# Dense products of a four-layer trunk in plain float32 instead of in three single-pass products

## The chip, the cores and the metric

The kernel runs on one core of a Trainium2 chip. The metric is the device time of one execution in microseconds (us); lower is better. Before the change it is 1484.35 us, the median of three runs (1482.13, 1484.35 and 1486.35).

A core has five engines with queues of their own: TensorE (PE) multiplies matrices into PSUM, VectorE (DVE) and ScalarE (ACT) work element by element, GpSimd (POOL) does a little of both, and SyncE (SP) issues transfers. The profile shows TensorE twice: PE is the multiplication, PEld the load of the stationary operand that goes ahead of it.

## The reference

512 tokens of width 1024 go through two layers, each a token mixer and a feed-forward block, with a residual addition after each of the four:

```
u = rms_norm(h, mixer_norm[0]);  h = h + swa_sink_attention(u)        # 16 heads of 64, window 128
u = rms_norm(h, ffn_norm[0]);    h = h + conv_glu_ffn(u)              # 1024 -> 2 x 3072 -> 1024
u = rms_norm(h, mixer_norm[1]);  h = h + gated_deltanet(u)            # 1024 -> 6176, 16 value heads, 2048 -> 1024
u = rms_norm(h, ffn_norm[1]);    h = h + conv_glu_ffn(u)
```

All inputs, weights and the output are float32. The dense products (attention in and out, the two feed-forward blocks, the DeltaNet's in and out projections) hold most of the arithmetic.

## The kernel before, in words

The residual `h` and every activation lie transposed: 128 features on the partitions, 512 tokens along the free axis, so a tensor of width 1024 is eight tiles of 128x512. A dense product takes one weight tile (128x1024, eight k tiles of 128x128) as stationary operand and the eight activation tiles as moving operand, and adds the eight k tiles up in one PSUM bank. Only the attention's input projection is turned round: there 128x128 pieces of the activation are stationary and 128x256 pieces of the weight move.

Both operands of a dense product are split in two float32r parts, float32r being a second format of four bytes: `hi` is the value rounded to it, `lo` what is left. `weight` (lines 128 to 139) loads a weight tile (`raw`), ScalarE makes `whi` (L137) and VectorE `wlo` (L138); the activations are split in `norm_split` (L192, L193), `normalise` (L223, L224) and `split` (L143, L144). `mm3` (L146 to L150) issues three products for each k tile, hi by hi, hi by lo and lo by hi. The weight pool has three slots for each of `raw`, `whi` and `wlo`.

The remaining products of the kernel have plain float32 operands before and after: attention scores (L515) and values (L546), and in the DeltaNet the per-head recurrence (L1013 to L1074). Transposes (L427, L537, L574) go through TensorE too.

The order of work is fixed when the program is built. The dense loops call `pump` once per one or two k tiles, and `pump` lets the waiting generators (attention lanes, the recurrence, the preparation of heads) emit their next piece, so small float32 products are strewn among dense ones. A scheduler then fixes each engine's order. All weights and most of the DeltaNet's reloads go through SP's queue in order. `live` counts the tiles taken from the pool of 36 activation tiles, and an epilogue (L1102) waits while there is no room.

Of the kernel before, what the change touches and what calls it, by code (L numbers as in the profile page):

```python
# [17 lines left out]
P = 128  # L18
T = 512
NB = 4  # L20
# [50 lines left out]
class Builder:  # L71
    def __init__(self, tc, ctx, ins, out):
# [3 lines left out]
        self.wp = pool("wp", 3)  # L76
# [44 lines left out]
    def a2(self, dt=F32R):  # L121
        return self.big.tile([P, T], dt, tag="a2", name="a2")
# [5 lines left out]
    def weight(self, src, cols=1024, parts=1):  # L128
        nc = self.nc
# [3 lines left out]
        w = cols // parts  # L133
        for i in range(parts):
            s = slice(i * w, (i + 1) * w)
# [3 lines left out]
        return hi, lo  # L139

    def split(self, src, hi, lo):
        nc = self.nc
        nc.scalar.copy(hi, src)  # L143
        nc.vector.tensor_tensor(lo, src, hi.bitcast(F32), op=ALU.subtract)  # L144

    def mm3(self, ps, w, x, first, last):  # L146
        mm = self.nc.tensor.matmul
# [4 lines left out]
    def dense(self, ps, hi, lo, x, n=KT, w=P, grain=2):  # L152
        for k in range(n):
            s = slice(k * w, (k + 1) * w)
# [31 lines left out]
    def norm_split(self, h, m, gain):  # L186
        nc = self.nc
        if m == 0:
            self.u = []
        hi, lo = self.a2(), self.a2()  # L190
        g = self.col(gain + m)
        nc.scalar.activation(hi, h, AF.Copy, scale=g)  # L192
        nc.vector.scalar_tensor_tensor(lo, h, g, hi.bitcast(F32), op0=ALU.mult, op1=ALU.subtract)  # L193
        self.u.append((hi, lo))
# [21 lines left out]
    def normalise(self, h, m, gain):  # L216

        nc = self.nc
        t = self.t2()
        nc.vector.tensor_tensor(t, h, self.bc, op=ALU.mult)  # L220
        hi, lo = self.a2(), self.a2()
        g = self.col(gain + m)
        nc.scalar.activation(hi, t, AF.Copy, scale=g)  # L223
        nc.vector.scalar_tensor_tensor(lo, t, g, hi.bitcast(F32), op0=ALU.mult, op1=ALU.subtract)  # L224
        self.u.append((hi, lo))


    def ffn(self, l, h, after):
        nc = self.nc
        u = self.u  # L230
        for third in range(3):
            act = []
            for j in range(third * 8, third * 8 + 8):
                gu = []
                for b in range(2):
                    hi, lo = self.weight(self.ins["up"][l, j, b])
                    ps = self.psum()
                    self.dense(ps, hi, lo, u)
                    gu.append(ps)
# [10 lines left out]
                nc.vector.tensor_tensor(t, t, y, op=ALU.mult)  # L250
                hi, lo = self.a2(), self.a2()
                self.split(t, hi, lo)
                act.append((hi, lo))
            for m in range(KT):
                hi, lo = self.weight(self.ins["down"][l, third, m])
                ps = self.psum()
                self.dense(ps, hi, lo, act)
# [138 lines left out]
    def attn(self, h, after):  # L396
# [38 lines left out]
        def lane(i):  # L435
# [3 lines left out]
            for x in range(NB + 2):  # L439
                if x >= 2:  # L440
# [3 lines left out]
                    if n == 0:  # L444
                        ao[i] = [(self.a2(), self.a2()) for _ in range(4)]
# [5 lines left out]
                    for g in range(4):  # L451
                        s = slice(n * P, (n + 1) * P)
                        hi, lo = ao[i][g]
                        self.split(po[:, g * P:(g + 1) * P], hi[:, s], lo[:, s])
# [19 lines left out]
        for c in range(6):  # L474
# [3 lines left out]
            for i, (t, k) in enumerate(order):  # L478
                ts = slice(t * P, (t + 1) * P)
                ps = pss[t // 2][:, (t % 2) * 256:(t % 2) * 256 + 256] if c else pss[t][:, :256]  # L480
                hi, lo = W[k // 4]
                s = slice(k % 4 * 256, k % 4 * 256 + 256)
                self.mm3(ps, (u[k][0][:, ts], u[k][1][:, ts]), (hi[:, s], lo[:, s]), k == 0, k == KT - 1)
# [7 lines left out]
        for i in range(2):  # L491
            self.until(lambda: ("o", i) in ready)
            for m in range(KT):
                hi, lo = self.weight(self.ins["wout"][i, m], 512)
                ps = self.psum()
                self.dense(ps, hi, lo, ao[i], 4, grain=1)
# [53 lines left out]
    def in_tile(self, j, u):  # L550
        hi, lo = self.weight(self.ins["gin"][j])
        ps = self.psum()
        self.dense(ps, hi, lo, u, grain=1)
# [26 lines left out]
    def gates(self, u, ready):  # L580
# [19 lines left out]
        hi, lo = self.weight(self.ins["gba"], 256)  # L600
        ps = self.psum()
        for k in range(KT):
            s = slice(k * 32, (k + 1) * 32)
            self.mm3(ps[:32], (hi[:, s], lo[:, s]), u[k], k == 0, k == KT - 1)
# [49 lines left out]
        self.rows2 = [self.a2().rearrange("p (n c) -> p n c", n=NB) for _ in range(2)]  # L654
# [16 lines left out]
    def gdn(self, h, hd, stack, after):  # L671
# [68 lines left out]
        self.live, self.started = 26, 0  # L740
# [23 lines left out]
        def part(ps, m, W, q, ks):  # L764
            hi, lo = W
            for k in ks:
                s = slice((m % 2 * 4 + k) * P, (m % 2 * 4 + k + 1) * P)
                self.mm3(ps, (hi[:, s], lo[:, s]), outs[4 * q + k], k == 0, k == 3)
# [8 lines left out]
        while r < len(rest) or g < 12:  # L777
            q = g // 4
            if r < len(rest) and (r < 3 * self.started or not have(4 * q + 4)):
                tile_in(rest[r])  # L780
                r += 1
                if r == len(rest):
                    self.live -= 16
            elif have(4 * q + 4):
# [11 lines left out]
                if g % 4 == 0:  # L796
                    self.live -= 8
# [281 lines left out]
    def epilogue(self, rx, hk, mo, o, ready, outs):  # L1079
# [22 lines left out]
        while self.live + 4 > 36:  # L1102
            yield 0.5
        self.live += 4
        for j in range(2):
            pt = self.turn(ob[j])
            V.scalar_tensor_tensor(z[:, j], pt, self.col(C_GN), z[:, j], op0=ALU.mult, op1=ALU.mult)
            hi, lo = self.a2(), self.a2()
            self.split(z[:, j], hi, lo)
            outs[2 * hk + j] = (hi, lo)  # L1110
# [68 lines left out]
```

## Time and profile before

| what | us |
|---|---|
| median of three runs | 1484.35 |
| profiled execution | 1481.57 |
| its span, first to last instruction | 1479.8 |
| PE busy | 1466.2 |
| PEld busy | 1216.8 |
| DVE busy | 913.7 |
| ACT busy | 636.3 |
| POOL busy | 104.7 |

Matmuls are pipelined: the next one starts while the last is still draining, so the duration of one in a row of the profile is longer than the time it takes from the engine. What a matmul takes is read from the distance between one start and the next.

### The profile page before, as it was taken

How to read it: one execution, taken by the hardware profiler on the slowest of the kernel's cores; microseconds unless marked ns; L12 is line 12 of the kernel's file. 1: busy time of each engine (PE TensorE's matmuls, PEld its weight loads, DVE VectorE, ACT ScalarE, POOL GpSimd, SP SyncE). 2: the span in 40 equal slices, each digit the busy share in tenths (PEclk: the TensorE clock that was granted, in tenths of full speed). 3: DMA queues.
4: the chain of work that ended last, by engine and by line, in shares of the span. 5: the costliest groups of instructions: out<-in, count | busy, mean ns of one | idle time of the engine just before them, and what ended most of it. 6: DMA issues, size and time to landing. Idle time of an engine off the chain costs nothing.

```text
span 1479.8 us, 20837 instructions
## 1 busy us (share of the span) xinstructions
PE 1466.2 (99%) x7972; PEld 1216.8 (82%) x7972; DVE 913.7 (62%) x1772; ACT 636.3 (43%) x1206; POOL 104.7 (7%) x141
## 2 busy tenths in 40 slices
PE   8999999999999999999999999999999999999998
PEld 8976688888888888878888888888888888888887
DVE  8778765446635556765685667767685535644552
ACT  6666643223313334667534454454453313322331
POOL 0122100000000000000112222230000000000000
PEclk9999999999999999999999999999999999999999
DMA  5201222222222233356866445453222222222231
GB/s 188 72 19 60 82 98 100 100 100 100 86 99 100 100 121 121 118 174 229 278 230 210 150 142 174 154 162 122 73 101 98 100 100 100 88 98 100 100 106 65
DMA packets 70940, 178.14 MB, mean 120 GB/s; under 512 B 17208, under 2 KB 23352, under 8 KB 70584
## 3 DMA queue, kind: packets, MB, share of 16 engines
q1 hardware_dynamic: 61128, 158.70, 32.1%
q10 hardware_dynamic: 7920, 16.27, 2.9%
q0 software_dynamic: 1792, 1.84, 0.7%
q8 instruction: 63, 1.03, 0.3%
q14 instruction: 37, 0.30, 0.1%
HBM read 150.46 MB, written 26.31 MB: 119 GB/s over the span
## 4 chain that ended last, share of the span: by engine, by line
PE 93%; DVE 3%; DMA 3%; ACT 1%; issue 1%; POOL 0%; SPq 0%; ACTq 0%; DVEq 0%; POOLq 0%
PE ps L148 27%; PE ps L149 27%; PE ps L150 27%; PE ps L574 1%; PE ps L1061 1%; PE ps L1074 1%; PE ps L515 1%; PE ps L546 1%; PE ps L1067 1%; PE ps L1056 1%; PE ps L1052 1%; DVE wlo L138 1%; ACT sc L524 1%; PE ps L537 1%; DMA vd<-t 1%; PE ps L1027 1%
## 5 line engine op out<-in xcount | busy, mean ns | idle before, releaser
L148 PE MATMUL ps<-a,whi 128*128 128x512 f32 x1736 | 688.9, 397 | 0.4 <-ACT a L143 0.4
L150 PE MATMUL ps<-a,wlo 128*128 128x512 f32 x1736 | 677.1, 390 | 0.0
L149 PE MATMUL ps<-a,whi 128*128 128x512 f32 x1736 | 676.9, 390 | 0.0
L137 ACT CAST whi<-raw 128x1024 fp32r<-128x1024 f32 (+1 forms) x239 | 242.4, 1015 | 434.1 <-PE ps L149 389.9
L148 PEld LDWEIGHTS ps<-a,whi 128*128 128x128 f32 x1736 | 325.4, 188 | 70.5 <-issue 2.5
L150 PEld LDWEIGHTS ps<-a,wlo 128*128 128x128 f32 x1736 | 325.2, 187 | 69.3
L149 PEld LDWEIGHTS ps<-a,whi 128*128 128x128 f32 x1736 | 325.8, 188 | 64.0 <-DVE a L144 0.2
L138 DVE TENSOR_TENSOR wlo<-raw,whi 128x1024 fp32r<-128x1024 f32 (+1 forms) x239 | 282.1, 1181 | 68.1 <-ACT whi L137 67.6
L258 DVE TENSOR_TENSOR h<-h,ps 128x512 f32<-128x512 f32 x48 | 33.0, 688 | 148.5 <-PE ps L150 148.5
L243 DVE TENSOR_TENSOR t<-ps,rbc 128x512 f32<-128x512 f32 x48 | 33.2, 691 | 109.3 <-PE ps L150 103.9
L249 DVE TENSOR_TENSOR t<-ps,rbc 128x512 f32<-128x512 f32 x48 | 33.2, 691 | 86.4 <-PE ps L150 86.3
L247 ACT ACTIVATE t<-t 128x512 f32<-128x512 f32 x48 | 30.4, 632 | 97.8 <-DVE t L246 97.8
L148 PE MATMUL ps<-whi,a 128*128 128x256 f32 x192 | 56.9, 298 | 1.2 <-ACT a L192 1.2
L149 PE MATMUL ps<-wlo,a 128*128 128x256 f32 x192 | 54.0, 283 | 1.2 <-DVE wlo L138 1.2
L150 PE MATMUL ps<-whi,a 128*128 128x256 f32 x192 | 53.1, 283 | 0.0
L954 POOL MEMSET TT<- 128x1024 f32 x8 | 7.7, 958 | 562.8 <-DMA Xd<-kd 554.9
L143 ACT CAST a<-t 128x512 fp32r<-128x512 f32 x48 | 29.9, 624 | 32.6 <-DVE t L250 32.6
L148 PEld LDWEIGHTS ps<-whi,a 128*128 128x128 f32 x192 | 36.6, 191 | 7.6 <-issue 4.9
L566 DVE SCALAR_TENSOR_TENSOR t<-ps,cols,t 128x511 f32<-128x511 f32 (+2 forms) x48 | 35.7, 744 | 7.1 <-ACT t L564 6.5
L244 ACT ACTIVATE t<-t,cols 128x512 f32<-128x512 f32 x48 | 38.9, 810 | 0.0
L528 POOL TENSOR_SCALAR sc<-sc,sm 128x256 f32<-128x256 f32 (+1 forms) x32 | 28.9, 913 | 128.2 <-DVE sm L526 65.1
L149 PEld LDWEIGHTS ps<-wlo,a 128*128 128x128 f32 x192 | 36.6, 191 | 1.4 <-DVE wlo L138 1.4
(252 smaller groups left out, 1472.5 us busy)
## 6 DMA issues: line engine op xcount, KB each, us to landing
raw<-in_up SPq DMA_DIRECT2D x96, 512.0 KB, 3.2
raw<-in_down SPq DMA_DIRECT2D x48, 512.0 KB, 3.2
raw<-in_gin SPq DMA_DIRECT2D x48, 512.0 KB, 3.6
raw<-in_gout SPq DMA_DIRECT2D x16, 512.0 KB, 3.5
raw<-in_win SPq DMA_DIRECT2D x10, 512.0 KB, 3.1
raw<-in_wout SPq DMA_DIRECT2D x16, 256.0 KB, 2.7
zd<-t ACTq DMA_DIRECT2D x16, 256.0 KB, 3.0
Dd<-D ACTq DMA_DIRECT2D x8, 512.0 KB, 2.7
```

The costliest lines, as they stand in the source:

```text
L137: nc.scalar.copy(hi[:, s], raw[:, s])
L138: nc.vector.tensor_tensor(lo[:, s], raw[:, s], hi[:, s].bitcast(F32), op=ALU.subtract)
L143: nc.scalar.copy(hi, src)
L148: mm(ps, w[0], x[0], start=first, stop=False)
L149: mm(ps, w[0], x[1], start=False, stop=False)
L150: mm(ps, w[1], x[0], start=False, stop=last)
L243: nc.vector.tensor_tensor(g, gu[0], self.bc, op=ALU.mult)
L244: nc.scalar.activation(y, g, AF.Identity, bias=self.col(C_FB + l * 24 + j), scale=self.col(cw + 2))
L247: nc.scalar.activation(y, y, AF.Silu)
L249: nc.vector.tensor_tensor(t, gu[1], self.bc, op=ALU.mult)
L258: nc.vector.tensor_tensor(h[m], h[m], ps, op=ALU.add)
L566: nc.vector.scalar_tensor_tensor(dst[:, i:], g[:, :T - i], self.col(cw + 3 - i), dst[:, i:], op0=ALU.mult, op1=ALU.add)
```

## The change

Weights and activations of dense products stay plain float32. `weight` only loads; there is no `split`, no `mm3`, and one product per k tile. The pool of weight tiles has six slots of one kind where it had three of each of three kinds. An activation takes one tile, not two, and the counts of `live` are halved. The core of the diff:

```diff
-        self.wp = pool("wp", 3)
+        self.wp = pool("wp", 6)
-    def a2(self, dt=F32R):
+    def a2(self, dt=F32):
     def weight(self, src, cols=1024, parts=1):
-        raw = self.wp.tile([P, 1024], F32, tag="raw", name="raw")
-        hi = self.wp.tile([P, 1024], F32R, tag="whi", name="whi")
-        lo = self.wp.tile([P, 1024], F32R, tag="wlo", name="wlo")
+        w = self.wp.tile([P, 1024], F32, tag="w", name="w")
...
-            nc.sync.dma_start(raw[:, s], src[:, s])
-            nc.scalar.copy(hi[:, s], raw[:, s])
-            nc.vector.tensor_tensor(lo[:, s], raw[:, s], hi[:, s].bitcast(F32), op=ALU.subtract)
+            self.nc.sync.dma_start(w[:, s], src[:, s])
...
-        mm(ps, w[0], x[0], start=first, stop=False)
-        mm(ps, w[0], x[1], start=False, stop=False)
-        mm(ps, w[1], x[0], start=False, stop=last)
...
-            self.mm3(ps, (hi[:, s], lo[:, s]), x[k], k == 0, k == n - 1)
+            self.nc.tensor.matmul(ps, w[:, k * P:(k + 1) * P], x[k], start=k == 0, stop=k == n - 1)
...
     def normalise(self, h, m, gain):
-        nc.vector.tensor_tensor(t, h, self.bc, op=ALU.mult)
...
-        nc.scalar.activation(hi, t, AF.Copy, scale=g)
-        nc.vector.scalar_tensor_tensor(lo, t, g, hi.bitcast(F32), op0=ALU.mult, op1=ALU.subtract)
+        self.nc.vector.scalar_tensor_tensor(x, h, self.col(gain + m), self.bc, op0=ALU.mult, op1=ALU.mult)
...
     def ffn(self, l, h, after):
-                nc.vector.tensor_tensor(t, t, y, op=ALU.mult)
-                hi, lo = self.a2(), self.a2()
-                self.split(t, hi, lo)
+                x = self.a2()
+                nc.vector.tensor_tensor(x, t, y, op=ALU.mult)
...
-        self.live, self.started = 26, 0
+        self.live, self.started = 18, 0
```

On TensorE, around the first step of the DeltaNet's chain (`S` is the state of a head, `qd` the decayed queries, `a2` the activation tiles, `whi`, `wlo` the parts of a weight), the kernel before has:

```order
L148 MATMUL ps_7241<-a2_5188,whi_7236 128x512
L149 MATMUL ps_7241<-a2_5189,whi_7236 128x512
L150 MATMUL ps_7241<-a2_5188,wlo_7237 128x512
L1052 MATMUL ps_7254<-S_7178,a2_5157 128x256
L1056 MATMUL ps_7179<-S_7178,qd_6486 128x128
L1056 MATMUL ps_7180<-S_7178,qd_6486 128x128
L148 MATMUL ps_7241<-a2_5246,whi_7236 128x512
L149 MATMUL ps_7241<-a2_5247,whi_7236 128x512
L150 MATMUL ps_7241<-a2_5246,wlo_7237 128x512
```

And at the same place after the change:

```order
L138 MATMUL ps_4277<-a2_2914,w_4275 128x512
L1023 MATMUL ps_4286<-S_4224,a2_2899 128x256
L1027 MATMUL ps_4225<-S_4224,qd_3800 128x128
L1027 MATMUL ps_4226<-S_4224,qd_3800 128x128
L138 MATMUL ps_4277<-a2_2948,w_4275 128x512
```

Three instructions of a k tile have become one, and the step of the chain stands after the same number of k tiles of its weight tile.

On VectorE, in the first feed-forward block (one column tile of the hidden layer: convolution, gate, product), the kernel before has:

```order
L243 TENSOR_TENSOR t2_3417<-ps_3361,rbc_2469 128x512
L138 TENSOR_TENSOR wlo_3464<-raw_3462,whi_3463 128x1024
L245 SCALAR_TENSOR_TENSOR t2_3418<-t2_3417,cols_78,t2_3418 128x511
L246 SCALAR_TENSOR_TENSOR t2_3418<-t2_3417,cols_78,t2_3418 128x510
L249 TENSOR_TENSOR t2_3424<-ps_3392,rbc_2469 128x512
L250 TENSOR_TENSOR t2_3424<-t2_3424,t2_3418 128x512
L138 TENSOR_TENSOR wlo_3509<-raw_3507,whi_3508 128x1024
L144 TENSOR_TENSOR a2_3428<-t2_3424,a2_3427 128x512
```

And after the change:

```order
L219 TENSOR_TENSOR t2_2097<-ps_2077,rbc_1733 128x512
L221 SCALAR_TENSOR_TENSOR t2_2098<-t2_2097,cols_78,t2_2098 128x511
L222 SCALAR_TENSOR_TENSOR t2_2098<-t2_2097,cols_78,t2_2098 128x510
L225 TENSOR_TENSOR t2_2104<-ps_2088,rbc_1733 128x512
L227 TENSOR_TENSOR a2_2106<-t2_2104,t2_2098 128x512
```

The two subtractions for the weights and the one for the activation are gone, and the product itself now writes the tile that the next dense product reads.

## Rows read from the trace of the kernel before

**Rows 1.** Page: span, then each engine's busy time, share and instructions.

```profile
span 1479.8 us, 20837 instructions
...
PE 1466.2 (99%) x7972; PEld 1216.8 (82%) x7972; DVE 913.7 (62%) x1772; ACT 636.3 (43%) x1206; POOL 104.7 (7%) x141
```

**Rows 2.** Page: shares of the chain that ended last, by engine.

```profile
PE 93%; DVE 3%; DMA 3%; ACT 1%; issue 1%; POOL 0%; SPq 0%; ACTq 0%; DVEq 0%; POOLq 0%
```

**Rows 3.** Page: costliest groups; columns are line, engine, tiles, count, busy us, mean ns, idle before.

```profile
L148 PE MATMUL ps<-a,whi 128*128 128x512 f32 x1736 | 688.9, 397 | 0.4 <-ACT a L143 0.4
...
L137 ACT CAST whi<-raw 128x1024 fp32r<-128x1024 f32 (+1 forms) x239 | 242.4, 1015 | 434.1 <-PE ps L149 389.9
L148 PEld LDWEIGHTS ps<-a,whi 128*128 128x128 f32 x1736 | 325.4, 188 | 70.5 <-issue 2.5
...
L138 DVE TENSOR_TENSOR wlo<-raw,whi 128x1024 fp32r<-128x1024 f32 (+1 forms) x239 | 282.1, 1181 | 68.1 <-ACT whi L137 67.6
...
L148 PE MATMUL ps<-whi,a 128*128 128x256 f32 x192 | 56.9, 298 | 1.2 <-ACT a L192 1.2
```

**Rows 4.** Windows of the span: us, each engine's busy us (count), PEclk, DMA share.

```profile
0.00:100.00 100.00, 94.93 (x716) 84.41 (x718) 79.97 (x344) 65.87 (x162) 14.46 (x20) 1.00 0.30 102
100.00:200.00 100.00, 97.66 (x504) 72.33 (x501) 71.88 (x232) 57.31 (x152) 14.66 (x16) 0.98 0.22 70
200.00:300.00 100.00, 100.00 (x443) 82.80 (x442) 54.11 (x68) 35.50 (x43) 0.00 (x0) 1.00 0.29 99
690.00:1085.00 395.00, 392.92 (x2815) 332.89 (x2815) 278.57 (x542) 187.25 (x402) 75.57 (x105) 1.00 0.53 170
```

**Rows 5.** Timeline of VectorE in the last feed-forward block: start, duration, [idle before].

```profile
1470.31 0.69 DVE L258 TENSOR_TENSOR h<-h,ps 128x512 f32<-128x512 f32 x1 [4.75 <-PE ps L150]
1475.74 0.69 DVE L258 TENSOR_TENSOR h<-h,ps 128x512 f32<-128x512 f32 x1 [4.75 <-PE ps L150]
```

**Rows 6.** Timeline of TensorE in the attention's input projection: first and eleventh k tile.

```profile
51.13 0.28 PE L148 MATMUL ps<-whi,a 128*128 128x256 f32 x1
...
54.73 0.28 PE L148 MATMUL ps<-whi,a 128*128 128x256 f32 x1
```

**Rows 7.** Timeline of TensorE in the DeltaNet's chain, first step.

```profile
805.94 0.59 PE L1052 MATMUL ps<-S,a 128*128 128x256 f32 x2
806.37 0.61 PE L1056 MATMUL ps<-S,qd 128*128 128x128 f32 x4
```

**Rows 8.** Timeline of TensorE in the DeltaNet, a later step: passes of 128 columns.

```profile
1014.15 0.61 PE L1056 MATMUL ps<-S,qd 128*128 128x128 f32 x4
1014.60 1.06 PE L1013 MATMUL ps<-a,a 128*128 128x128 f32 x8
```

**Rows 9.** Timeline of TensorE in the attention: values, four passes of 512 columns.

```profile
71.05 1.26 PE L546 MATMUL ps<-pT,v 128*64 128x512 f32 x4
72.23 0.39 PE L148 MATMUL ps<-whi,a 128*128 128x256 f32 x1
```

**Rows 10.** Windows at the start and the attention's end (columns as in Rows 4).

```profile
0.00:6.00 6.00, 4.51 (x10) 3.20 (x10) 1.39 (x5) 2.40 (x3) 0.21 (x4) 1.00 0.61 210
7.00:25.00 18.00, 15.55 (x124) 14.90 (x124) 16.48 (x57) 14.26 (x27) 0.00 (x0) 1.00 0.69 235
148.00:157.00 9.00, 7.04 (x37) 3.51 (x36) 6.39 (x27) 7.69 (x27) 3.20 (x4) 0.99 0.13 35
157.00:161.00 4.00, 3.97 (x15) 1.93 (x13) 0.44 (x2) 1.24 (x3) 0.53 (x1) 0.60 0.00 0
```

**Rows 11.** Timeline of TensorE at the start: warm-up, first dense product.

```profile
1.49 4.63 PE L1129 MATMUL ps<-t 128*128 128x256 f32 x10 [1.49 <-DVE gcol L343]
6.80 0.39 PE L148 MATMUL ps<-whi,a 128*128 128x256 f32 x1 [0.67 <-ACT a L192]
```

**Rows 12.** Timeline of TensorE, a wait of the input projection.

```profile
21.77 0.39 PE L149 MATMUL ps<-wlo,a 128*128 128x256 f32 x1 [1.20 <-DVE wlo L138]
```

**Rows 13.** Page: weight loads; KB each, median us from issue to landing.

```profile
raw<-in_up SPq DMA_DIRECT2D x96, 512.0 KB, 3.2
```

More of the change, by code (lines that the diff above doesn't have):

```diff
@@ L189, in norm_split @@
             self.u = []
-        hi, lo = self.a2(), self.a2()
[L191 to L194, printed above, removed]
+        x = self.a2()
+        nc.scalar.activation(x, h, AF.Copy, scale=self.col(gain + m))
+        self.u.append(x)
     def norm_end(self, wait=2):
@@ L235, in ffn @@
                 for b in range(2):
-                    hi, lo = self.weight(self.ins["up"][l, j, b])
+                    w = self.weight(self.ins["up"][l, j, b])
                     ps = self.psum()
-                    self.dense(ps, hi, lo, u)
+                    self.dense(ps, w, u)
                     gu.append(ps)
@@ L249, in ffn @@
                 nc.vector.tensor_tensor(t, gu[1], self.bc, op=ALU.mult)
[L250 to L253 removed]
+                x = self.a2()
+                nc.vector.tensor_tensor(x, t, y, op=ALU.mult)
+                act.append(x)
             for m in range(KT):
[L255 removed]
+                w = self.weight(self.ins["down"][l, third, m])
                 ps = self.psum()
[L257 removed]
+                self.dense(ps, w, act)
                 nc.vector.tensor_tensor(h[m], h[m], ps, op=ALU.add)
@@ L444, in lane @@
                     if n == 0:
-                        ao[i] = [(self.a2(), self.a2()) for _ in range(4)]
+                        ao[i] = [self.a2() for _ in range(4)]
                     po = self.psum()
@@ L493, in attn @@
             for m in range(KT):
-                hi, lo = self.weight(self.ins["wout"][i, m], 512)
+                w = self.weight(self.ins["wout"][i, m], 512)
                 ps = self.psum()
-                self.dense(ps, hi, lo, ao[i], 4, grain=1)
+                self.dense(ps, w, ao[i], 4, grain=1)
                 nc.vector.tensor_tensor(h[m], h[m], ps, op=ALU.add)
@@ L550, in in_tile @@
     def in_tile(self, j, u):
-        hi, lo = self.weight(self.ins["gin"][j])
+        w = self.weight(self.ins["gin"][j])
         ps = self.psum()
-        self.dense(ps, hi, lo, u, grain=1)
+        self.dense(ps, w, u, grain=1)
         return ps
@@ L599, in gates @@
         nc.scalar.copy(self.selr, sel[:, 4:])
-        hi, lo = self.weight(self.ins["gba"], 256)
+        w = self.weight(self.ins["gba"], 256)
         ps = self.psum()
         for k in range(KT):
-            s = slice(k * 32, (k + 1) * 32)
-            self.mm3(ps[:32], (hi[:, s], lo[:, s]), u[k], k == 0, k == KT - 1)
+            nc.tensor.matmul(ps[:32], w[:, k * 32:(k + 1) * 32], u[k], start=k == 0, stop=k == KT - 1)
         ba = self.t2()
@@ L653, in gates @@
         V.tensor_copy(bt, pt[:, 0:P])
-        self.rows2 = [self.a2().rearrange("p (n c) -> p n c", n=NB) for _ in range(2)]
+        self.rows2 = [self.a2(F32R).rearrange("p (n c) -> p n c", n=NB) for _ in range(2)]
         hi, lo = self.rows2
@@ L782, in gdn @@
                 if r == len(rest):
-                    self.live -= 16
+                    self.live -= 8
             elif have(4 * q + 4):
@@ L796, in gdn @@
                 if g % 4 == 0:
-                    self.live -= 8
+                    self.live -= 4
             else:
@@ L1101, in epilogue @@
         yield 2
-        while self.live + 4 > 36:
+        while self.live + 2 > 36:
             yield 0.5
-        self.live += 4
+        self.live += 2
         for j in range(2):
             pt = self.turn(ob[j])
[L1107 to L1110, printed above, removed]
+            x = self.a2()
+            V.scalar_tensor_tensor(x, pt, self.col(C_GN), z[:, j], op0=ALU.mult, op1=ALU.mult)
+            outs[2 * hk + j] = x
             ready.add(("o", 2 * hk + j))
```

32 lines of the change are left out of this document (9 added, 23 removed).

## The prediction

> **What bounds the kernel now.** I read the busy times first: PE 1466.2 of a span of 1479.8 us, the next engine, DVE, 913.7 [rows 1]. The reader is to see that one engine fills the span, and that what the change takes from ACT and DVE lies beside it. The chain of waits says the same: 93% of it is PE, 3% DVE [rows 2]. Then the busy times by stretch, since an average could hide a stage with another limit: in a feed-forward stretch PE is busy 100.00 of 100 us, in the DeltaNet 392.92 of 395, and only in the attention does it stand still, 5.07 us in the first 100 and 2.34 in the next [rows 4]. So the time follows what TensorE spends, and the whole question is what one k tile costs in either form. A busy share can't say that, since matmuls overlap; the distance between starts can.
>
> *Three float32r products, 512 columns.* Two successive residual additions in the last feed-forward block end the wait for PE 1475.74 - 1470.31 = 5.43 us apart [rows 5]. Between them lie eight k tiles of three products, so one product takes 5.43 / 24 = 0.2263 us and a k tile 0.679. At 2.4 GHz, the level that granted clock 1.00 stands for, 512 columns at one clock each are 0.2133; the other 0.013 is overhead per product.
>
> *Three float32r products, 256 columns.* In the attention's input projection the same product of the first and of the eleventh k tile start 3.60 us apart [rows 6]: 0.360 per k tile.
>
> *One float32 product.* The kernel before has plain float32 products already, in the recurrence. The order shows one instruction at L1052 and two at L1056; the trace shows two and four [rows 7], so each float32 product runs as two passes. From the first pass of L1052 to the first of L1056 it is 806.37 - 805.94 = 0.43 us: two passes of 256 columns, 0.215 each, two clocks a column. The four passes of 128 columns at L1056 take 1014.60 - 1014.15 = 0.45, 0.1125 each [rows 8], again two clocks a column (0.107) and little else, although each loads its own 128 columns of weights. So a float32 product costs four clocks a column, where the three parts cost three.
>
> **The change part by part.**
>
> *512-column k tiles.* There are 1736, the same count in each of the three lines [rows 3]. The trace has no full-width float32 product of 512 columns; I take twice the one of 256, 0.86 us. The low end is four clocks a column without overhead, 4 x 512 / 2.4 GHz = 0.853; the high end gives each of the two passes the 0.013 overhead of a float32r product of that width, 2 x (0.427 + 0.013) = 0.879. I take 0.86, since L1052 has full width, float32 and dense neighbours, and its overhead was 0.002 a pass. Per k tile +0.181, in all 1736 x 0.181 = +314.2 us; ends 1736 x 0.174 = +302.6 and 1736 x 0.200 = +347.9.
>
> The Trainium skill, "FP8 and Floating Point Precision", section "TensorE Precision Notes", says that true FP32 takes four passes through the array. Two passes at two clocks a column is in time what it says. Taken as four full instructions at the 0.2263 seen here it would be 0.905 a k tile, more than the row shows.
>
> *256-column k tiles.* 192 [rows 3], from 0.360 to the measured 0.43: +13.4 us (low end 0.427: +12.8).
>
> *Casts and subtractions.* L137 (242.4 us on ACT), L138 (282.1 on DVE) [rows 3] and the splits of activations go. PE covers them nearly everywhere, so the work itself returns nothing. What returns is where PE waited for them: 1.20 us for `wlo` in the input projection [rows 12], the start, where the first dense product begins at 6.80, 0.67 after the warm-up's end, behind an ACT cast of the weight and one of the activation [rows 11], and some of the DeltaNet's 2.08 us of idle time [rows 4]. At most it is all the idle time of the three stretches, 5.07 + 2.34 + 2.08 = 9.5 us; at least nothing, since behind a cast the loads or the warm-up may be late next. I take 5, most of it from the first 25 us: -5. The idle time in the attention's end belongs to the softmax, and stays.
>
> *Six weight slots for three times three.* Before, the cast of a tile waited for the products three tiles back, and its raw load for the cast three tiles back; now the load waits for the products six tiles back. That is the same distance, so SP's queue, in which the recurrence's reloads stand behind weight loads, is held no longer than before. A weight load lands in 3.2 us [rows 13], and eight k tiles will take 6.9 instead of 5.4 us: hidden with more room. If that cover were gone, PE would wait at most one landing per tile; I count nothing.
>
> *Order, buffers.* Chain steps stand after as many k tiles as before, and these are 27% longer, so whoever waits for the recurrence has more cover. One tile per activation and halved `live` loosen a limit that no row shows as binding: nothing.
>
> The sum: 314.2 + 13.4 - 5 = +322.6 on the profiled span, 1479.8 + 322.6 = 1802.4. The profiled execution was 1.8 us above its span (1481.57) and 2.8 below the median of the runs (1484.35), so the median to expect is 1802.4 + 1.8 + 2.8 = 1807. Low ends: 302.6 + 12.8 - 9.5 = +305.9, 1787 on the profiled execution's own scale. High ends: 347.9 + 13.4 = +361.3, 1846 on that of the median.
>
> **The rivals.**
>
> *A. A float32 pass costs one clock a column: faster.* Then a k tile is two passes of 0.2263 = 0.453 where it was 0.679: 1736 x 0.226 = -393, the 192 others -23, with the 5 above -421, about 1063 us. For it speaks the only float32 row of 512 columns: four passes of L546 take 72.23 - 71.05 = 1.18 us, 0.295 each [rows 9], well under 0.43. Against it: those have 64 output rows (128 by 64 in the row) and alternate between two halves of the array, so two can run beside each other; L1052 has 128 and takes two clocks a column. It decides if the pass pitch of 512 full-width columns is under 0.34. 3%.
>
> The Trainium skill, "Perfetto Trace Analysis", section "Engine Utilization", halves the output rate for FP32_LOW_HIGH. Read as half for the whole product it is this rival; read per pass, with two passes, it is the forecast. The trace agrees with the second reading, 0.215 us for 256 columns.
>
> *B. The clock falls under plain float32.* For it: at the attention's end, where the last softmax is waited for and hardly a dense product runs, the granted clock falls from 0.99 to 0.60 of full speed [rows 10]. Against it: PE was busy only 7.04 of the 9 us before, so it had gaps, which dense float32 has not. And at the start ten float32 passes alone took 4.63 us [rows 11], 0.46 each and so the lower of the two levels (0.215 at L1052, the same width), whatever the clock column says there, and the next stretch had 1.00 [rows 10]: float32 alone brought the clock up. If it fell throughout to the lower level, 1.2 GHz, every dense product would take twice its forecast: 1736 x 0.86 + 192 x 0.43 = 1576 more, about 3380. 3%.
>
> *C. Four passes with overhead each.* The price is four times 0.2263, 0.905 a k tile, 0.48 for 256 columns: 1736 x 0.226 + 192 x 0.12 - 5 = +410, about 1895. L1052 speaks against it (0.215 a pass, two records a product). 4%.
>
> *D. Weight loads come out from under the products.* Two loads for each product, 0.188 each at the PEld mean [rows 3], none of it covered: 1928 x 0.376 = 725 more, about 2530. Against: the 0.1125 pitch of L1056 holds a pass of 0.107 and the load for the next, so 0.006 of a load at most shows there. 2%.
>
> **How the numbers follow.** Forecast 87%, A 3%, B 3%, C 4%, D 2%, anything else 1%. A measurement tells 0.3%, some 4.5 us, from no change. Only A is faster: 0.03; no case but the unnamed ends within 0.3%: 0.01; slower 0.96. The range is the forecast's own, 1787 to 1846; with the cases outside it some 13% is left out.
>
> **What will show it.** Right: two recorded matmuls per dense instruction (3472 at 512 columns), starts 0.43 apart in a feed-forward stretch; residual additions 6.9 us apart instead of 5.43; clock 1.00; PE near 99%, DVE less busy by more than the 282 of L138, and no new releaser before PE's idle time. The first dense product before 6.8 us and no wait near 21.8 would confirm the 5. Wrong: a pitch of 0.22 (A) or of 0.45 and more (C, D), a granted clock under 0.95 (B), or idle PE in a feed-forward stretch, which would say that the loads are late.

## The result, and the profile after

The changed kernel takes 1795.4 us, the median of four runs (1794.31 to 1798.01), against 1483.6 of the kernel before in the same runs: 1.210 times as long, 95% interval 1.208 to 1.213. The forecast was 1807, range 1787 to 1846. The profiled execution is the slowest of the four (1798.01, span 1796.2), 2.6 us above the median; against the profiled execution of before, its span is 316.4 us longer, where +322.6 was forecast.

The page after, busy times and the chain's shares:

```profile
span 1796.2 us, 16018 instructions
...
PE 1784.9 (99%) x6044; PEld 902.3 (50%) x6044; DVE 590.8 (33%) x1397; ACT 364.7 (20%) x895; POOL 100.6 (6%) x141
...
PE 95%; DVE 2%; ACT 2%; DMA 1%; issue 0%; POOL 0%; ACTq 0%; DVEq 0%; POOLq 0%; SPq 0%
```

One engine still fills the span [rows 1], and its share of the chain has gone from 93 to 95% [rows 2]. DVE is 323 us less busy, ACT 272, and hardly any of that shortened the kernel, as the experiments show. The dense groups of the page after (line, engine, operation, tiles, count, busy us, mean ns, idle before):

```profile
L138 PE MATMUL ps<-a,w 128*128 128x512 f32 x3200 | 1395.0, 593 | 0.4 <-ACT a L428 0.4
...
L739 PE MATMUL ps<-a,w 128*128 128x512 f32 x256 | 118.2, 595 | 0.0
...
L456 PE MATMUL ps<-w,a 128*128 128x256 f32 x384 | 92.8, 392 | 1.5 <-ACT a L174 1.5
```

The order has one instruction per k tile, the trace has two records: 3200 + 256 and the 16 of the gates' small product make 3472, twice 1736, and 384 is twice 192 [rows 3]. By stretch (us, then busy us and count of PE, PEld, DVE, ACT, POOL, then granted clock, DMA share, GB/s; the last one lies in the DeltaNet):

```profile
0.00:100.00 100.00, 97.00 (x480) 78.64 (x480) 51.83 (x265) 45.17 (x120) 10.11 (x16) 1.00 0.30 99
100.00:200.00 100.00, 95.95 (x384) 51.16 (x384) 48.77 (x203) 44.80 (x150) 17.46 (x20) 0.98 0.15 45
200.00:300.00 100.00, 100.00 (x247) 45.23 (x246) 28.20 (x50) 15.48 (x22) 0.00 (x0) 1.00 0.27 84
850.00:1300.00 450.00, 449.77 (x2406) 257.81 (x2404) 214.40 (x467) 129.87 (x328) 73.00 (x105) 1.00 0.48 145
```

The feed-forward stretch is full, with 247 records in 100 us where there were 443 [rows 4]. The clock column has 1.00 but for the attention's end, where it is 0.98 as before: plain float32 keeps the clock. (The first 14 us are an exception, below.) Two residual additions at the end, which answer to [rows 5]:

```profile
1785.31 0.69 DVE L233 TENSOR_TENSOR h<-h,ps 128x512 f32<-128x512 f32 x1 [6.18 <-PE ps L138]
1792.17 0.69 DVE L233 TENSOR_TENSOR h<-h,ps 128x512 f32<-128x512 f32 x1 [6.18 <-PE ps L138]
```

They are 6.86 us apart instead of 5.43: 0.858 us per k tile, 0.429 per pass of 512 columns, where the forecast had 0.86 and 0.43.

The last residual addition of each stage shows where the time came from. In the kernel before, attention, first feed-forward block, DeltaNet (the second of the two merged additions, at 1082.79):

```profile
184.72 0.68 DVE L497 TENSOR_TENSOR h<-h,ps 128x512 f32<-128x512 f32 x1
...
577.39 0.69 DVE L258 TENSOR_TENSOR h<-h,ps 128x512 f32<-128x512 f32 x1 [2.05 <-PE ps L150]
...
1082.19 1.28 DVE L772 TENSOR_TENSOR h<-h,ps 128x512 f32<-128x512 f32 x2
```

And after:

```profile
209.57 0.69 DVE L470 TENSOR_TENSOR h<-h,ps 128x512 f32<-128x512 f32 x1 [1.36 <-PE ps L138]
...
705.76 0.69 DVE L233 TENSOR_TENSOR h<-h,ps 128x512 f32<-128x512 f32 x1 [4.79 <-PE ps L138]
...
1295.99 0.69 DVE L743 TENSOR_TENSOR h<-h,ps 128x512 f32<-128x512 f32 x1 [1.36 <-PE ps L739]
```

| stage | before, us | after, us | difference | k tiles times difference | left |
|---|---|---|---|---|---|
| attention | 184.7 | 209.6 | +24.9 | 64 x 0.1795 + 192 x 0.071 = 25.2 | -0.3 |
| feed-forward 1 | 392.7 | 496.2 | +103.5 | 576 x 0.1795 = 103.4 | 0.1 |
| DeltaNet | 505.4 | 590.2 | +84.8 | 520 x 0.1795 = 93.3 | -8.5 |
| feed-forward 2 | 393.0 | 496.2 | +103.2 | 103.4 | -0.2 |

0.1795 us is what a k tile costs more in the feed-forward blocks, where TensorE waits for nothing. It is taken from those two rows, so they agree with it by construction; the distances of residual additions, 6.86 and 5.43 us for eight k tiles, give 0.179. So the price of a float32 product explains the result but for 8.9 us. In the table nearly all of these are in the DeltaNet, but the attention's 0.3 is a balance of larger terms. The prediction had looked for 5 us, most of them in the first 25.

The start is where it went wrong. ScalarE at the start of the kernel before:

```profile
2.15 1.28 ACT L137 ACT_TABLE_LOAD   x1 [2.15 <-issue]
4.41 0.62 ACT L137 CAST whi<-raw 128x512 fp32r<-128x512 f32 x1 [0.98 <-DMA raw<-in_win]
```

ScalarE and TensorE at the start of the kernel after:

```profile
5.57 1.28 ACT L174 ACT_TABLE_LOAD   x1 [5.57 <-DMA h<-in_xT]
6.86 1.59 ACT L174 ACTIVATE a<-h,cols 128x512 f32<-128x512 f32 x2
```

```profile
7.64 2.93 PE L456 MATMUL ps<-w,a 128*128 128x256 f32 x6 [1.50 <-ACT a L174]
```

The first dense product comes at 7.64, later than the 6.80 of before [rows 11]. ScalarE's first work used to be the cast of a weight, and its table load ran while that weight was on its way; now the first work waits for a tile of `h`, the table load stands behind that wait, and its 1.28 us lie on the path.

A second loss at the start belongs to this execution, not to the kernel. The row has six passes of 256 columns in 2.93 us: their starts are 0.43 us apart, the lower of the clock's two levels (1.2 GHz), and stay so until 13.77; from there on they are 0.215 apart (2.4 GHz). The clock column says 1.00 in both stretches, but the counts of passes in 5 us differ, 13 and 25:

```profile
8.00:13.00 5.00, 5.00 (x13) 3.92 (x13) 0.69 (x1) 5.00 (x9) 0.00 (x0) 1.00 0.82 284
14.00:19.00 5.00, 5.00 (x25) 4.41 (x24) 4.55 (x11) 2.64 (x6) 0.00 (x0) 1.00 0.76 274
```

Fourteen starts took 6.13 us where 14 x 0.2157 = 3.02 would have done, so some 3.1 us went there. In the first trial with the attention's value products (below), whose start is the same, the first eight passes take 1.99 us:

```profile
7.37 1.99 PE L456 MATMUL ps<-w,a 128*128 128x256 f32 x8 [1.79 <-ACT a L174]
```

The attention of that run ends at 207.4 and not 209.6. Of the other kernels below with this start, three have the higher level from the first dense product on, and one falls back to the lower from 8.1 to 11.4 us; why the level comes at another time in each execution isn't shown. Without that loss the attention would have grown by about 3 us less than its k tiles, and the span of 1796.2 would be about 1793, near the 1792.5 of two executions that were not profiled.

### The profile page after: what moved, and what is told of

It is laid out like the page before. It is cut to its first block, busy times and chain, and to the rows that moved or that the text cites. A ratio compares the mean times of both kernels' runs of the same rounds, so it can differ in the third digit from the quotient of the medians.

```text
span 1796.2 us, 16018 instructions
## 1 busy us (share of the span) xinstructions
PE 1784.9 (99%) x6044; PEld 902.3 (50%) x6044; DVE 590.8 (33%) x1397; ACT 364.7 (20%) x895; POOL 100.6 (6%) x141
## 4 chain that ended last, share of the span: by engine, by line
PE 95%; DVE 2%; ACT 2%; DMA 1%; issue 0%; POOL 0%; ACTq 0%; DVEq 0%; POOLq 0%; SPq 0%
PE ps L138 76%; PE ps L739 6%; PE ps L456 4%; ACT sc L497 1%; PE ps L547 1%; DVE sc L491 1%; PE ps L1032 1%; PE ps L1045 1%; PE ps L1038 1%; PE ps L1027 1%; PE ps L1023 1%; DVE sc L501 1%; PE ps L992 0%; PE ps L998 0%; PE ps L984 0%; PE ps L822 0%
## 5 line engine op out<-in xcount | busy, mean ns | idle before, releaser
L138 PE MATMUL ps<-a,w 128*128 128x512 f32 x3200 | 1395.0, 593 | 0.4 <-ACT a L428 0.4
L138 PEld LDWEIGHTS ps<-a,w 128*128 128x128 f32 x3200 | 600.2, 190 | 722.3 <-issue 715.6
L233 DVE TENSOR_TENSOR h<-h,ps 128x512 f32<-128x512 f32 x48 | 33.0, 688 | 283.4 <-PE ps L138 283.4
L739 PE MATMUL ps<-a,w 128*128 128x512 f32 x256 | 118.2, 595 | 0.0
L456 PE MATMUL ps<-w,a 128*128 128x256 f32 x384 | 92.8, 392 | 1.5 <-ACT a L174 1.5
L456 PEld LDWEIGHTS ps<-w,a 128*128 128x128 f32 x384 | 72.4, 196 | 16.8 <-issue 5.2
L739 PEld LDWEIGHTS ps<-a,w 128*128 128x128 f32 x256 | 45.2, 190 | 40.6 <-issue 38.3
L221 DVE SCALAR_TENSOR_TENSOR t<-t,cols,t 128x511 f32<-128x511 f32 x48 | 36.0, 750 | 40.5 <-ACT t L220 40.5
L222 DVE SCALAR_TENSOR_TENSOR t<-t,cols,t 128x510 f32<-128x510 f32 x48 | 36.0, 750 | 1.7
L227 DVE TENSOR_TENSOR a<-t,t 128x512 f32<-128x512 f32 x48 | 33.2, 692 | 7.6 <-ACT t L223 2.8
L497 ACT ACTIVATE sc<-sc,nm 128x256 f32<-128x256 f32 (+1 forms) x64 | 30.0, 469 | 21.9 <-DVE es L494 13.4
L743 DVE TENSOR_TENSOR h<-h,ps 128x512 f32<-128x512 f32 x32 | 21.9, 685 | 35.4 <-PE ps L739 35.1
L491 DVE CUSTOM_DVE_ANT_0 sc<-ps,band,rows 128x256 f32<-128x256 f32 (+1 forms) x64 | 26.4, 441 | 11.3 <-PE ps L488 11.3
## 6 DMA issues: line engine op xcount, KB each, us to landing
w<-in_up SPq DMA_DIRECT2D x96, 512.0 KB, 3.5
w<-in_down SPq DMA_DIRECT2D x48, 512.0 KB, 3.6
w<-in_gin SPq DMA_DIRECT2D x48, 512.0 KB, 4.1
w<-in_gout SPq DMA_DIRECT2D x16, 512.0 KB, 4.0
w<-in_win SPq DMA_DIRECT2D x10, 512.0 KB, 4.3
Dd<-D ACTq DMA_DIRECT2D x8, 512.0 KB, 3.7
```

The lines of the kernel that those rows point to most:

```text
L138: self.nc.tensor.matmul(ps, w[:, k * P:(k + 1) * P], x[k], start=k == 0, stop=k == n - 1)
L221: nc.vector.scalar_tensor_tensor(y[:, 1:], g[:, :T - 1], self.col(cw + 1), y[:, 1:], op0=ALU.mult, op1=ALU.add)
L222: nc.vector.scalar_tensor_tensor(y[:, 2:], g[:, :T - 2], self.col(cw), y[:, 2:], op0=ALU.mult, op1=ALU.add)
L456: nc.tensor.matmul(ps, u[k][:, ts], W[k // 4][:, s], start=k == 0, stop=k == KT - 1)
L491: nc.vector.tensor_tensor_reduce(sc[:, g, :W], pss[g % 2][:, (g // 2) * W:(g // 2) * W + W], self.band[:, 2 * P - W:], 1.0, sink[:, g:g + ...
L497: nc.scalar.activation(sc[:, g, :W], sc[:, g, :W], AF.Exp, bias=nm[:, g:g + 1], accum_out=sm[:, g:g + 1])
```

## The experiments

Ten kernels were run, in four groups by question. A "stage" is the time from one stage's last residual addition to the next stage's.

### Do the casts cost time of their own?

In the first kernel the weights of the kernel after are cast as before, for nobody:

```diff
+        hi = self.wp.tile([P, 1024], F32R, tag="whi", name="whi", bufs=2)
+        lo = self.wp.tile([P, 1024], F32R, tag="wlo", name="wlo", bufs=1)
...
             self.nc.sync.dma_start(w[:, s], src[:, s])
+            self.nc.scalar.copy(hi[:, s], w[:, s])
+            self.nc.vector.tensor_tensor(lo[:, s], w[:, s], hi[:, s].bitcast(F32), op=ALU.subtract)
```

> The kernel after the change, in which each weight tile is still cast to hi on ScalarE and subtracted to lo on VectorE as before, 218 + 21 tiles, though no product reads the two. Tests whether the casts cost time by themselves, and where the 8.4 us come from by which the DeltaNet stage grew less than its k tiles do (from 505.4 to 590.2 us where 520 k tiles would add 93.2). Theory 1 (TensorE covers the casts everywhere; the 8.4 us belong to the float32r products themselves, which follow each other more slowly beside float32 ones): span within 3 us of the 1796.2 of the kernel after, DeltaNet stage 589 to 592. Theory 2 (the chain's steps on ScalarE and VectorE queued behind casts, and TensorE waited for them): DeltaNet stage 596 to 600, span 1801 to 1806.

Its span is 1796.3, that of the kernel after. The ends of the first feed-forward block and of the DeltaNet:

```profile
703.50 0.69 DVE L237 TENSOR_TENSOR h<-h,ps 128x512 f32<-128x512 f32 x1 [0.39 <-PE ps L142]
...
1296.02 0.69 DVE L747 TENSOR_TENSOR h<-h,ps 128x512 f32<-128x512 f32 x1 [0.39 <-PE ps L743]
```

The DeltaNet takes 592.5, 2.3 us more than without the casts: half a microsecond outside what theory 1 gave, far from theory 2. In four other profiles whose DeltaNet is that of the kernel after it takes 590.2 to 590.8, so the 2.3 stand out of the spread. The span is equal all the same because the attention ends 2.3 us earlier here: the casts bring the table load forward again, and the higher clock comes at 7.6 us. The ratio to the kernel before is 1.214 (1.212 to 1.215); its interval overlaps that of the kernel after, but each of the four executions (1798.3 to 1803.3) is slower than each of the four of the kernel after (1794.3 to 1798.0). So the casts most likely cost a few microseconds; how many, the medians, 1800.3 and 1795.4, don't settle.

The second kernel takes VectorE's part away from the kernel before:

```diff
-            nc.vector.tensor_tensor(lo[:, s], raw[:, s], hi[:, s].bitcast(F32), op=ALU.subtract)
-        return hi, lo
+        return hi, hi
```

> The kernel before, with three float32r products per k tile, but without VectorE's subtraction for the weights: the third product takes hi of the weight in place of lo, so the low part of the weights is left out of the result. Takes some 282 us off VectorE and leaves TensorE's work as it was. Theory 1 (casts are covered): span 1476 to 1480, only the 1.2 us wait for wlo in the attention goes, DeltaNet stage within 2 us of 505.4. Theory 2 (VectorE's subtractions delay the chain): DeltaNet stage 497 to 501, span 1470 to 1474.

Ten runs have a median of 1483.9, ratio 1.000 (0.999 to 1.001). 282 us of VectorE's work are worth nothing that the runs can tell. The profiled execution, at a span of 1485.0, was above the 1476 to 1480 of theory 1: its DeltaNet took 511.3, with 6.2 us of idle TensorE instead of 2.1 and a granted clock of 0.66 from 770 to 775 us, behind a wait of 2.2 us, that the kernel before did not have, so that stage can't be compared closer.

### Is it the change of format?

What is left, then, are the float32r products themselves. The trace of before has the hint: behind a float32 product the dense ones follow each other more slowly, and in the feed-forward blocks there are almost none. Two kernels put one there, behind each weight tile, in the kernel before and in the kernel after:

```diff
+    def insert(self):
+        d = self.psum()
+        self.nc.tensor.matmul(d[:, :P], self.ident, self.ident, start=True, stop=True)
...
                     self.dense(ps, hi, lo, u)
+                    self.insert()
...
                 self.dense(ps, hi, lo, act)
+                self.insert()
```

> The kernel before, with one small float32 product (identity by identity, 128 columns, two passes, read by nobody) behind each of the 144 weight tiles of the feed-forward blocks, where TensorE waits for nothing. With its twin it measures what it costs to go from float32r to float32 and back, apart from any wait. Two passes alone are 2 x 0.1125 = 0.225 us. If changing between the formats costs extra (in the DeltaNet of before the trace has about 0.045 at the first dense product behind a float32 one and 0.03 over the next six): 0.28 to 0.31 us an insertion, each feed-forward stage 392.8 + 72 x 0.295 = 414. If only waits made the DeltaNet's float32r products late: 0.225 an insertion, stage 409.

> The same insertion in the kernel after, where its neighbours are float32 too. If the change of format is what costs: 0.225 to 0.265 us an insertion, each feed-forward stage 496.2 + 72 x 0.225 to 0.265 = 512.4 to 515.3, and less than in the twin by 0.03 to 0.07 each. If a small product costs the same wherever it stands: the same as the twin within 0.01.

The last residual additions of the attention and of the first feed-forward block, in the kernel before with the insertion:

```profile
185.86 0.67 DVE L503 TENSOR_TENSOR h<-h,ps 128x512 f32<-128x512 f32 x1
...
598.38 0.69 DVE L264 TENSOR_TENSOR h<-h,ps 128x512 f32<-128x512 f32 x1 [2.33 <-PE ps L150]
```

That is 412.5 us, 19.85 more than the 392.67 of before, 0.276 us for each of 72 insertions. The same with the insertion in the kernel after:

```profile
207.57 0.69 DVE L476 TENSOR_TENSOR h<-h,ps 128x512 f32<-128x512 f32 x1 [1.36 <-PE ps L138]
...
719.61 0.69 DVE L239 TENSOR_TENSOR h<-h,ps 128x512 f32<-128x512 f32 x1 [5.01 <-PE ps L138]
```

512.0 us, 15.85 more than 496.19, 0.220 each: what two passes of 128 columns cost, and no more. The same small product costs 0.056 us more between float32r products than between float32 ones; the second feed-forward blocks of the two runs give the same, 0.275 and 0.220. (The kernel before came out a little under its 414, the kernel after a little under its range's 512.4.) The timelines show where. First before with the insertion (L162), from the last dense product ahead of it to the second behind it, and the tenth; then after (L145):

```profile
306.23 0.40 PE L150 MATMUL ps<-a,wlo 128*128 128x512 f32 x1
306.46 0.38 PE L162 MATMUL ps<-ident 128*128 128x128 f32 x2
306.60 0.48 PE L148 MATMUL ps<-a,whi 128*128 128x512 f32 x1
306.92 0.40 PE L149 MATMUL ps<-a,whi 128*128 128x512 f32 x1
...
308.77 0.39 PE L148 MATMUL ps<-a,whi 128*128 128x512 f32 x1
```

```profile
308.19 0.38 PE L145 MATMUL ps<-ident 128*128 128x128 f32 x2
308.41 7.03 PE L138 MATMUL ps<-a,w 128*128 128x512 f32 x16
315.28 0.38 PE L145 MATMUL ps<-ident 128*128 128x128 f32 x2
```

The starts of the first two dense products behind it are 0.32 apart instead of 0.226, but that is hardly a loss: the first of them starts only 0.14 behind the insertion's start, where two passes take 0.22. From the last product ahead of it to the second behind it 0.69 us pass, and 0.226 + 0.22 + 0.226 is 0.67. The loss builds up behind: the next eight starts take 308.77 - 306.92 = 1.85 us instead of 1.81. Averaged over the insertions it is 0.01 us at the second dense product and 0.06 at the eleventh, from which on the distance is 0.226 again. After the change the tile of sixteen passes starts 0.22 behind the insertion and takes its usual 6.87. So a small float32 product makes the float32r products that follow slower for a while; why they are slower isn't shown.

In the DeltaNet of before, the timeline has 131 places where a dense product follows another kind, and 131 x 0.056 would be 7.3 of the 8.5 us. That is an upper estimate, since at 106 of them nine dense products or fewer follow before another small one: summed by the length of each stretch, with what the insertion had lost by then, it is some 5 us. With the 2.3 of the casts some 7 to 8 of the 8.5 are accounted for, by estimate; the rest is open, and the 8.5 is itself no firmer than a couple of microseconds, as the same stage, unchanged, took 507.6 in the kernel before with the insertion. (Not all of the other products are float32, as the description of the kernel has it: 48 in the DeltaNet, L828 to L830 in the kernel after, are float32r in both kernels, and 8 of the 131 places follow one.)

The attention of before has 51 such places, about 2 us by the same sum. With 1.2 us less idle time of TensorE behind the start, the wait for `wlo` [rows 12] among it, they answer the 0.8 and the 3.1 lost at the start, and the attention's balance comes out near nothing.

### Is the start's loss the table load?

One copy of a column on ScalarE behind the issue of the first two transfers of `h`, in the kernel after:

```diff
+            if self.first and m == 1:
+                early = self.small.tile([P, 1], F32, name="early")
+                nc.scalar.activation(early, self.ones, AF.Copy)
```

> The kernel after, with one copy of a single column on ScalarE ahead of its first real work, right behind the two transfers of h that it issues. In the kernel after the table load of ScalarE starts at 5.57 us, when h has landed, takes 1.28 and puts the first dense product at 7.64; before, the weight's cast drew it to 2.15. If the table load alone made the start late: first dense product at 6.2 to 6.6, span 1.0 to 1.4 us shorter. If h's landing or the warm-up sets it: first product unchanged at 7.4 or later.

```profile
2.15 1.28 ACT L1105 ACT_TABLE_LOAD   x1 [2.15 <-issue]
...
5.06 0.72 ACT L174 ACTIVATE a<-h,cols 128x512 f32<-128x512 f32 x1 [1.41 <-DMA h<-in_xT]
```

```profile
5.92 3.26 PE L456 MATMUL ps<-w,a 128*128 128x256 f32 x10
```

The table load is back at 2.15, and the first dense product at 5.92, 1.72 us earlier than in the kernel after, and more than expected: the wait for `h` ended at 5.06 here. The span is 1792.8, 3.4 less, all of it in the attention, which ends at 206.1 instead of 209.6. Part of that is the clock: here it reaches the higher level at 7.55, and not at 13.77. Against the first trial with the value products, which has the late table load and the early clock (attention's end at 207.4), 1.3 us are left, within the 1.0 to 1.4 of the expectation; that is one profile each. What is shown is the cause of the late start.

### What a pass costs, and the rivals

Rival A rested on the attention's value products, with 64 output rows. In the kernel after they still start in pairs, eight passes in 1.94 us:

```profile
92.32 1.94 PE L519 MATMUL ps<-pT,v 128*64 128x512 f32 x8
```

The first trial put the two key heads' products one behind the other in the program:

```diff
-                    for b in range(len(both[0])):
-                        for j in range(2):
+                    for j in range(2):
+                        for b in range(len(both[0])):
```

> The kernel after, in which the attention's value products of the two key heads no longer alternate: both blocks of the first head, then both of the second, in the six groups of eight passes. Tests rival A's only evidence, the four passes of 512 columns with 64 output rows in 1.18 us. If two such products run beside each other because they go to two halves of the array, at two clocks a column each: a group of eight passes takes 2.6 to 3.2 us where it took 1.94, the span some 4 to 7 us more. If 64 output rows by themselves cost one clock a column: groups stay at 1.9, span unchanged within 2 us.

```profile
90.04 1.95 PE L519 MATMUL ps<-pT,v 128*64 128x512 f32 x8
```

Nothing changed, against what I expected of the halves. Taken alone that spoke for rival A's reading. The second trial therefore put dense products in between:

```diff
+                    for j in range(2):
                         for b in range(len(both[0])):
-                        for j in range(2):
                             self.attn_values(n, 2 * i + j, both[j], v, po, b)
+                        if j == 0:
+                            yield 0.5
```

> The kernel after, in which dense products stand between the attention's value products of the first and of the second key head, so that never both heads' products (the two halves of the 64-row outputs) are queued side by side. The alternating order and the one head after the other had both given pairs of passes that start together every 0.43 us. If it is the two passes of one 64-row product that run beside each other: two products of one head (four passes) take 1.08 us, passes in pairs. If it is two products in the two halves: passes one by one, 0.43 apart, four in about 1.9 us.

```profile
90.94 1.93 PE L521 MATMUL ps<-pT,v 128*64 128x512 f32 x4
92.80 1.13 PE L458 MATMUL ps<-w,a 128*128 128x256 f32 x4
```

Four passes of one head take 1.93 us, one by one, some 0.44 apart. So a pass of 64 output rows costs two clocks a column like any other, and the pairs are two products in two halves of the array. That they still pair in the first trial, with two products of one half ahead of the other half's, means that the chip doesn't keep to the program's order there (the built program of that trial does have two products of one half, then two of the other); how far it looks ahead I did not test.

If two halves run beside each other, could dense products gain by it?

```diff
-            self.nc.tensor.matmul(ps, w[:, k * P:(k + 1) * P], x[k], start=k == 0, stop=k == n - 1)
+            for c in range(2):
+                self.nc.tensor.matmul(ps[c * 64:c * 64 + 64], w[:, k * P + c * 64:k * P + c * 64 + 64], x[k], start=k == 0, stop=k == n - 1, skip_group_check=True)
```

> The kernel after, in which each dense product in the loop of eight k tiles is given as two products of 64 output rows each. If a 64-row product's two passes fill the array side by side and nothing more can run with them: 2 x 0.43 per k tile, residual additions 6.9 us apart, span within 15 us of 1796. If the two halves could run beside each other on top of that: 0.43 per k tile, residual additions 3.5 us apart, span near 1080, faster than both kernels.

```profile
699.52 5.32 PE L139 MATMUL ps<-a,w 128*64 128x512 f32 x24
```

24 passes, twelve pairs, in 5.32 us: eleven steps of 0.43 and the last pass of 0.59. Two halves fill the array and cost what one full product costs. The feed-forward blocks are unchanged (496.8), so this is no faster kernel; the DeltaNet is 22.8 us longer (613.0), with TensorE busy throughout, for which I have no tested cause, and takes the span to 1818.5, outside the 15 us I had given.

Width and weight loads:

```diff
+            for c in range(2):
+                self.nc.tensor.matmul(ps[:, c * 256:c * 256 + 256], w[:, k * P:(k + 1) * P], x[k][:, c * 256:c * 256 + 256], start=k + c == 0, stop=k == n - 1 and c == 1)
```

> The kernel after, in which each of the 1728 dense products of 512 columns is given as two of 256 columns, so that passes and weight loads are twice as many and columns the same. If a pass costs two clocks a column and its weight load is covered: a k tile goes from 0.858 (6.87 us between residual additions, eight k tiles) to 4 x 0.2157 = 0.863, residual additions 6.90 us apart, span +6 to +10. If weight loads show (rival D: 0.188 each): at least +0.1 per added load, span +170 or more.

```profile
325.43 0.69 DVE L234 TENSOR_TENSOR h<-h,ps 128x512 f32<-128x512 f32 x1 [5.42 <-PE ps L139]
332.34 0.69 DVE L234 TENSOR_TENSOR h<-h,ps 128x512 f32<-128x512 f32 x1 [6.22 <-PE ps L139]
```

6.91 us between residual additions, against 6.87. Twice the loads and passes at the same columns cost 0.005 us per k tile. The span, 1801.0, is only 4.8 longer, but the kernel after lost 3.1 at its start to the clock and this run did not: the two feed-forward blocks and the DeltaNet together are 8.2 longer (2.9, 2.9 and 2.4), within the 6 to 10 expected. Rival D is out.

Last, the kernel before with two of its three products:

```diff
         mm(ps, w[0], x[0], start=first, stop=False)
-        mm(ps, w[0], x[1], start=False, stop=False)
         mm(ps, w[1], x[0], start=False, stop=last)
```

> The kernel before without the second of its three products (hi of the weight by lo of the activation is left out of the result); all casts and subtractions stay. Prices one float32r pass and shows what is late next. If every stage stays bound by TensorE: feed-forward stages 392.7 - 576 x 0.2263 = 262 us each, DeltaNet 505 - 118 = 387, span about 1064. If the DeltaNet becomes bound by VectorE (there 356 us busy of 505) and the chain: feed-forward stages 262, DeltaNet 400 or more, span 1075 to 1110.

It takes 1183.7 us, ratio 0.797 (0.796 to 0.799), and both theories were wrong about the whole. The first feed-forward block, the DeltaNet, the second block:

```profile
173.40:438.00 264.60, 264.21 (x1168) 217.78 (x1169) 210.71 (x270) 133.71 (x163) 0.00 (x0) 1.00 0.49 154
438.00:907.00 469.00, 402.32 (x2827) 333.15 (x2826) 352.83 (x693) 261.71 (x594) 75.76 (x105) 0.94 0.57 179
907.00:1177.80 270.80, 267.05 (x1167) 219.95 (x1167) 203.50 (x259) 122.77 (x147) 0.00 (x0) 0.98 0.45 141
```

The first block gives what the product costs (264.6 against 262). The DeltaNet takes 469 us, not 387, nor a little over 400: PE is idle for 67 of them, and the granted clock is 0.94: 0.50 from 620 to 661 us, where PE is busy for 10.5 of 41, and 0.96 to 1.00 in the rest. VectorE, which I had named, is busy 353 of 469, so it isn't full. The largest single wait in this stage:

```profile
PE ps L986 <- DMA NT<-Nd: 29.0, 2, 27.5
```

It is for a reload from HBM in the chain that solves the heads' small triangular systems, 27.5 us once. With a third of the dense work gone, the serial steps of this stage no longer lie beside it; that this is why the reload is waited for is argued, no run tests it. So rival A would not have come to 1063 either, at least with the casts: the price per pass was right, and the rest of its sum assumed that TensorE stays the limit.

## Why the prediction was right

Slower by the price of a pass: right, and it is nearly the whole result. *Two passes at two clocks a column* were read from a product of 256 columns between dense neighbours [rows 7]; the 512-column pass came out at 0.429 instead of 0.43. Over 1736 k tiles that is 2.6 us less than forecast, 311.6 for 314.2. The high end, which gave each pass the overhead of a float32r product, was not needed: a float32 pass carries 0.002 us, not 0.013. *256-column k tiles*: 13.7 for 13.4.

*Casts and subtractions, -5*: wrong in place and cause, and short by 3.9 us. The sum it stood for was -8.9. In the attention, where I had put most of it, only 0.3 was left. The wait near 21.8 did go, as forecast, but the first dense product came at 7.64 and not before 6.8, since the table load moved onto the path; that the removal of an engine's first instruction also removes what had drawn its table load forward was the step I missed. Another 3.1 us went to the late clock of the profiled execution. Of the 8.5 in the DeltaNet the casts have about 2.3 at most; the larger part came from a term I did not have, float32r products that are slower behind float32 ones. What nearness there is between -5 and -8.9 is luck. I had bounded that stage's gain by PE's idle time, 2.08 us [rows 4], and that bound does not hold: a matmul's record of 0.39 us covers a start distance of 0.226 [rows 3, 5], so 0.1 us lost between two starts shows as busy.

*The median.* 1795.4 lies 11.6 under the forecast's 1807, further than the 6.2 of the spans: I had put the median 2.8 above the profiled execution, as it was before, and this time it lay 2.6 below, which the late clock explains.

*Weight slots, order, buffers: nothing.* Borne out for the weight slots by the feed-forward stretches, where TensorE is busy 100.00 of 100 us; in the DeltaNet it is idle for 0.2 us, where it was 2.1. None of the runs tested the slots, the order or the halved `live` by themselves.

Rivals: A is refuted, and what spoke for it is explained by halves of the array. B is refuted by a granted clock of 1.00 and passes 0.429 apart in the feed-forward blocks. But its reading that the ten warm-up passes bring the clock up did not hold in the profiled execution, where the lower level lasted until 13.77 us and cost 3.1. C and D are refuted by the pitch of 0.429 and by the doubled loads. The four-pass rule of the Trainium skill ("FP8 and Floating Point Precision", section "TensorE Precision Notes") holds in time, four clocks a column: 0.853 of 0.858 us. By that rule and the float32r rows alone, three passes against four, one would have said 1.33 and not 1.26 per k tile; the difference is the float32r product's overhead of 0.013, which the rule doesn't have.

## What to carry to other kernels

When one engine fills the span, count what each form costs it, from the distance between starts of the nearest like instruction: three float32r products take 0.68 us for 512 columns, one float32 product 0.86, and the 595 us of other engines' work that the change saved were worth a few microseconds beside it. Read a gap between pipelined instructions from start to start, not from busy or idle time, and look for places where two formats alternate. When an instruction goes that was first on its engine, ask what it had set up. Before a microsecond at the start is put down to the change, compare the distances between starts there: two executions of the same code can run it at different clocks.

## What the runs showed that I had not expected

- A small float32 product between float32r products costs TensorE 0.056 us beyond its own passes, nearly all of it in the ten products that follow (about 0.231 between starts instead of 0.226).
- A float32r product of 512 or of 256 columns takes 0.013 us more than its columns, a float32 pass 0.002. What makes the difference was not tried.
- Two products of 64 output rows each, in two halves of the array, run beside each other even when the program has another product of the first half between them.
- Dense work sets not only the pace: with two products in place of three the DeltaNet stage fell to a granted clock of 0.94 (0.50 in the 41 us where TensorE was busy for 10.5).
- The same start ran at the lower clock until 13.77 us in the profiled execution of the kernel after, and at the higher from the first dense product on in four other profiles with that start.
